# An encoder layer on one core: the MLP of 1,024 tokens as one chunk in two passes instead of two chunks of 512 in one

## The chip, the cores and the metric

The kernel runs on one core of one Trainium2 chip. The metric is the device time of one execution in microseconds (us), taken over several runs; lower is better. The core has a matrix engine (TensorE, in the profile PE for matmuls and PEld for weight loads), VectorE (DVE), ScalarE (ACT), GpSimd (POOL), and SyncE (SP), whose queue issues nearly all DMAs here. Data sits in SBUF (128 partitions), matmuls accumulate in PSUM (eight banks of 512 fp32 columns), and everything larger goes to DRAM.

## The reference

One layer of an encoder, applied to a prompt of 512 tokens and a sample of 1,024 tokens with the same weights, in fp32. Cut to the part that the change touches:

```
def _layer(h, ...):
    ...                                   # norm, projection, attention and pooling, output projection
    m = _rmsnorm(h, norm_mlp_g)           # h: tokens x 1024
    h = h + jnp.square(jax.nn.relu(m @ w_up)) @ w_down      # w_up 1024 x 4096, w_down 4096 x 1024
    gate = jax.nn.sigmoid(_rmsnorm(h, norm_ple_g) @ w_ple_gate)
    h = h + gate * (p_i @ w_ple_proj)     # then a final norm
```

## The kernel before

The 1,536 tokens are three chunks `c` of 512: chunk 0 is the prompt, chunks 1 and 2 are the sample. After attention come the MLP (about 548 to 1,574 us of the profile) and the gate with the final norm.

**Numbers in two parts.** Every fp32 operand of a large matmul is split: a high part, rounded by a ScalarE copy to the type fp32r that TensorE takes, and a low part, the rest, made by a subtraction on VectorE or GpSimd. A product then takes three matmuls (high by high, high by low, low by high; `three`, L103).

**Seven products for eight.** Both MLP products use Winograd's form of Strassen's scheme: each operand is cut into four blocks, and seven products of sums and differences of blocks give the four blocks of the result. `UP` and `DOWN` (L1204) are the orders in which the seven are taken.

**First product** (`m @ w_up`, relu, square). The 4,096 columns of `w_up` are 16 pairs `g` of 256; `pairs` (L1209) is a list of 48, chunk by chunk. The token side is cut in halves, so the moving operand of each matmul has 256 columns. The combinations of `m` are made once per chunk (`make_m`, L678), stored in DRAM (`mo_d`), and read back by `load_mo` (14 tiles per chunk). A pair's weight combinations are made by `Pair.feed` (L949) from the raw weights. Chunk 0 makes them for all 16 pairs and stores those of 15 (`KEPT`) in `kept_d`; chunks 1 and 2 read them back (`fetch`, L945) and make them only for pair 0. `Pair.product` (L991) is one product of 12 matmuls; `run7` (L1065) is a pair of chunk 1 or 2: seven products, with PSUM results combined on VectorE and ScalarE (`sc.copy(t, x)`, `u2`, `u4`, the relus and squares) into the tiles `X` of a `Double`.

**Second product.** For chunk 0 it is a plain product (`Pair.down`, L999: four pieces per pair, each of 12 matmuls of 512 columns), run by `between` one pair late. For chunks 1 and 2 two pairs make a `Double` (L1112) with seven products in Strassen's form (`down`, L1171: 24 matmuls of 256 columns, into `d0` or `d1`, two PSUM banks each); `weights` (L1128) makes the combinations of `w_down` anew for each of the 16 doubles, `inputs` (L1153) those of `X`. A double's results are added to the running sums `HS` by VectorE (`out`, L1188, the row L1196 of the profile).

**The order.** One loop over `pairs` (L1620) writes out the order. After each of a pair's products `after(i)` (L1649) takes one step of the weight stream `feeding`, of `inputs` and of `weights`, and one `step` of the side work in `chores` (squares and norms, `make_m`, `finishing`, `raise_late`, `gating`). For chunks 1 and 2, after every second product of pair n one product of the double before is put into the PE order; its sums are taken by `flush`. So first and second product of a chunk alternate on PE. PE, ACT, DVE and POOL run in the order of the program; SP's DMAs are ordered by a scheduler, but a `load` (L55) not before its turn in PE's order. Tiles come from a pool of 49 slots of SBUF (`NSLOT`, L32); a new tile waits until one is free.

**After the MLP.** `gate` (L1699) runs for chunk 0, chunk 1, and chunk 2 in two halves. Chunk 0's gate alternates on PE with the last double's products (`next_down`).

Of the kernel before, what the change touches and what calls it, by code (L numbers as in the profile page):

```python
# [18 lines left out]
P = 128  # L19
# [16 lines left out]
def encoder_layer(ctx, tc, xT, xn, xr, pT, w1, w2, w_pool, w_out, w_up, w_down, w_gate, w_proj,  # L36
# [587 lines left out]
    def rsqrt_rows(parts, w, name):  # L624
# [11 lines left out]
        if name in ("g0", "g1"):  # L636
            yield
# [14 lines left out]
        if name in ("g0", "g1"):  # L652
            yield from wait(2)
# [3 lines left out]
        yield from wait({"f20": 4, "g2": 8, "f00": 7, "f10": 4}.get(name, 3))  # L657
# [6 lines left out]
    wr_d = dram.tile([P, CH], F32, name="wr_d")  # L664
# [13 lines left out]
    def make_m(c, et, el):  # L678
# [15 lines left out]
        for b in range(2):  # L694
# [17 lines left out]
            def keep(i, j, out, b=b):  # L712
                sy.dma_start(mo_d[c][i][j][:, 2 * b:2 * b + 2], as32(out[:, j]))
                if j:
                    made.add((c, i, b))
# [19 lines left out]
        if c == 2:  # L735
            sy.dma_start(wr_d, acc[:, 1])
# [6 lines left out]

    def load_mo(c, i):
# [3 lines left out]
        for j in range(2):  # L748
            load(as32(MO[c, i][j]), mo_d[c][i][j])
# [7 lines left out]

    def quarters(t):
        return t.rearrange("p (a b) -> p a b", b=HF)

    def scaled(c, nm, a):
        t = quarters(HS[c][nm][:, a * CH:(a + 1) * CH])
        ve.tensor_tensor(t, t, ws[c][:, TOK[nm[1]]].unsqueeze(1).to_broadcast([P, 2, HF]), op=ALU.mult)

    def rest(c, nm):
        r = slot([P, D], F32, f"rest{c}{nm}")
        for a in range(2):
            load(quarters(r[:, a * CH:(a + 1) * CH]), h_d[c][2 * (int(nm[0]) - 1) + a][:, :, TOK[nm[1]]])
        return r
# [10 lines left out]
    HALVES = (slice(0, CH), slice(CH, D))  # L780

    def raise_late(c):
        w = slot([P, CH], F32, f"wr{c}")
        load(w, wr_d)
        r = {}

        def fetch(nm):
            r[nm] = rest(c, nm)
            yield

        def scale(nm):
            for part in HALVES:
                t = quarters(r[nm][:, part])
                ve.tensor_tensor(t, t, w[:, TOK[nm[1]]].unsqueeze(1).to_broadcast([P, 2, HF]), op=ALU.mult)
                yield

        def add(nm):
            for part in HALVES:
                gp.tensor_tensor(HS[c][nm][:, part], HS[c][nm][:, part], r[nm][:, part], op=ALU.add)
                yield  # L800

        yield from staged(("22", "11", "12", "21"), fetch, scale, add)

    def squares(c, acc):

        sqs = {}

        def square(nm):
            sqs[nm] = slot([P, 4, HF], F32, f"sqh{c}{nm}")
# [1091 lines left out]
```

## Time and profile before

| | |
|---|---|
| time, median of 3 runs | 1727.47 us (1727.32 to 1727.59) |
| the profiled execution: its time | 1728.79 us |
| its span, first to last instruction | 1726.5 us |
| PE busy | 1713.6 us (99%) |
| DVE, ACT, POOL busy | 1253.0, 888.9, 1073.5 us (73%, 51%, 62%) |
| granted TensorE clock, mean | 0.997 of full |
| DMA | 400.69 MB, mean 232 GB/s |

The rows shown below come from several views of this one profiled execution. The page gives totals per engine. A row of the groups reads: line, engine, operation, tiles out<-in, shapes, count | busy time together, mean ns of one | idle time before them and what ended it. A row of the timeline reads: start, duration, engine, line, operation, count of neighbours that were merged. A row of the stages gives, for a stretch of time, each engine's busy time and instruction count, then the granted clock, the DMA engines' share and the rate. Matmuls overlap in the pipeline (the listed mean is a latency), so the price of one is read from the distance between starts, not from its duration.

### The profile page before, as it was taken

What the parts mean: (1) busy time and instruction counts of PE and PEld (TensorE: products, weight loads), DVE (VectorE), ACT (ScalarE), POOL (GpSimd) and SP (SyncE); (2) the same over time, 40 slices, a digit from 0 to 9 for tenths busy, and PEclk for the clock granted to TensorE, in tenths of its full rate; (3) what the DMA queues carried; (4) which work ended last, traced back from release to release, by engine and by line L of the source; (5) the groups of instructions that cost most, each with busy time, mean ns of one, the idle gap of its engine ahead of it and who ended that gap; (6) DMA issues with size and microseconds to landing.
All of it is one profiled execution on the core that took longest, in us unless ns stands there. A gap on an engine that the chain in (4) does not pass through costs nothing.

```text
span 1726.5 us, 31311 instructions
## 1 busy us (share of the span) xinstructions
PE 1713.6 (99%) x11716; PEld 1573.6 (91%) x11716; DVE 1253.0 (73%) x1724; ACT 888.9 (51%) x1607; POOL 1073.5 (62%) x871
## 2 busy tenths in 40 slices
PE   9999999999999999999999999999999999999998
PEld 7888888888889888888999999999999999998898
DVE  6776765788887568777657778777778788665665
ACT  6444355667884546555435455544454445543233
POOL 2495983534666656777547877776688675653522
PEclk9999999999999999999999999999999999999998
DMA  7464655120429986979797778799777789743012
GB/s 260 144 220 168 238 185 194 37 99 14 151 109 356 322 299 246 391 264 370 274 394 287 265 276 319 260 330 354 264 238 267 261 328 388 267 167 116 13 50 98
DMA packets 137495, 400.69 MB, mean 232 GB/s; under 512 B 14592, under 2 KB 27264, under 8 KB 137344
## 3 DMA queue, kind: packets, MB, share of 16 engines
q1 hardware_dynamic: 136784, 398.30, 63.2%
q8 instruction: 93, 1.52, 0.4%
q14 instruction: 58, 0.48, 0.1%
q10 hardware_dynamic: 560, 0.40, 0.1%
HBM read 280.41 MB, written 118.23 MB: 231 GB/s over the span
## 4 chain that ended last, share of the span: by engine, by line
PE 55%; DMA 4%; DVE 4%; ACT 1%; issue 1%; POOL 1%; POOLq 0%; SPq 0%; DVEq 0%; ACTq 0%
PE pd L49 25%; PE pz L49 7%; PE px L49 7%; PE pq L49 7%; PE pg L49 5%; PE py L49 3%; PE pj L49 1%; DMA kept_d<-w 1%; DMA mo<-mo_d 1%; DMA rest<-h_d 1%; DMA we<-in_w_down_dram 1%; DVE h L1769 1%; DMA w<-kept_d 1%; DMA mo_d<-mm 0%; DVE s L1735 0%
## 5 line engine op out<-in xcount | busy, mean ns | idle before, releaser
L49 PE MATMUL pd<-ta,v 128*128 128x256 f32 x2688 | 337.9, 282 | 0.1
L49 PEld LDWEIGHTS pd<-ta,v 128*128 128x128 f32 x2688 | 327.9, 189 | 0.7 <-POOL v L1145 0.3
L1145 POOL TENSOR_TENSOR v<-we,v 128x512 fp32r<-128x512 f32 x128 | 185.4, 1469 | 91.0 <-DVE ta L1165 30.0
L1145 POOL TENSOR_TENSOR v<-vs,v 128x512 fp32r<-128x512 f32 x96 | 130.9, 1385 | 102.2 <-DVE c L1168 33.7
L49 PE MATMUL pd<-r,wd 128*128 128x512 f32 x768 | 189.3, 394 | 0.9 <-DVE r L1062 0.9
L49 PE MATMUL z<-w,x 128*128 128x512 f32 (+1 forms) x864 | 173.6, 358 | 0.0
L536 POOL TENSOR_SCALAR pr<-pr,rr 128x1024 f32<-128x1024 f32 (+1 forms) x96 | 94.5, 984 | 126.5 <-DVE rr L534 67.4
L49 PEld LDWEIGHTS pd<-r,wd 128*128 128x128 f32 x768 | 139.8, 188 | 29.9 <-DVE r L1062 2.1
L49 PEld LDWEIGHTS z<-w,x 128*128 128x128 f32 x864 | 143.2, 189 | 25.5 <-ACT w L163 0.6
L1165 DVE TENSOR_TENSOR ta<-c,ta 128x512 fp32r<-128x512 f32 x112 | 112.7, 1006 | 73.7 <-ACT ta L1163 62.3
L956 POOL TENSOR_TENSOR w<-ws,w 128x512 fp32r<-128x512 f32 x72 | 104.5, 1452 | 94.3 <-ACT w L955 86.4
L49 PE MATMUL px<-mo,w 128*128 128x256 f32 x1152 | 152.9, 282 | 0.0
L49 PE MATMUL pq<-mo,w 128*128 128x256 f32 x1152 | 152.5, 281 | 0.3 <-DMA w<-kept_d 0.2
L49 PE MATMUL pz<-mo,w 128*128 128x256 f32 x1152 | 152.3, 281 | 0.4 <-DVE u L1092 0.4
L49 PEld LDWEIGHTS pz<-mo,w 128*128 128x128 f32 x1152 | 145.4, 189 | 3.8 <-DVE u L1092 0.6
L49 PEld LDWEIGHTS px<-mo,w 128*128 128x128 f32 x1152 | 144.7, 189 | 2.2 <-ACT u L1077 0.6
L49 PEld LDWEIGHTS pq<-mo,w 128*128 128x128 f32 x1152 | 143.1, 189 | 1.0 <-issue 0.7
L49 PE MATMUL pg<-hg,wg 128*128 128x512 f32 (+1 forms) x768 | 141.1, 338 | 0.3 <-DVE hg L1487 0.3
L546 ACT CAST pt<-tp 128x512 fp32r<-128x512 f32 x160 | 88.0, 590 | 100.9 <-PE tp L53 100.2
L49 PEld LDWEIGHTS pg<-hg,wg 128*128 128x128 f32 x768 | 119.3, 188 | 17.1 <-DVE hg L1487 0.5
L547 DVE TENSOR_TENSOR pt<-tp,pt 128x512 fp32r<-128x512 f32 x160 | 104.1, 683 | 40.9 <-ACT pt L546 40.8
L520 DVE TENSOR_REDUCE nm<-S 128x1 f32<-128x1024 f32 (+1 forms) x96 | 100.2, 1043 | 26.6 <-PE S L49 26.1
(272 smaller groups left out, 3512.4 us busy)
## 6 DMA issues: line engine op xcount, KB each, us to landing
w<-kept_d SPq DMA_DIRECT2D x210, 512.0 KB, 5.9
kept_d<-w SPq DMA_DIRECT2D x105, 512.0 KB, 4.7
we<-in_w_down_dram SPq DMA_DIRECT2D x64, 512.0 KB, 6.7
mo_d<-mm SPq DMA_DIRECT2D x84, 256.0 KB, 6.2
mo<-mo_d SPq DMA_DIRECT2D x42, 512.0 KB, 10.2
wur<-in_w_up_dram SPq DMA_DIRECT2D x36, 512.0 KB, 6.5
wdr<-in_w_down_dram SPq DMA_DIRECT2D x32, 512.0 KB, 6.3
h_d<-h SPq DMA_DIRECT2D x16, 512.0 KB, 2.9
```

What stands on the lines that cost most here:

```text
L49: last_pe[0] = nc.tensor.matmul(*a, **k).ins
L520: ve.tensor_reduce(nm, S[:, :nch * CH], axis=AX.X, op=ALU.max, negate=True)
L536: gp.tensor_scalar(p, p, rr, 1.0, op0=ALU.mult, op1=ALU.mult)
L546: sc.copy(self.pt[kt][:, 0], tp)
L547: ve.tensor_tensor(self.pt[kt][:, 1], tp, as32(self.pt[kt][:, 0]), op=ALU.subtract)
L956: gp.tensor_tensor(t[:, 1], x, as32(t[:, 0]), op=ALU.subtract)
L1145: ins = gp.tensor_tensor(lo[:, p], src[:, p], as32(hi[:, p]), op=ALU.subtract).ins
L1165: last_ve[0] = ve.tensor_tensor(t[:, 1], x, as32(t[:, 0]), op=ALU.subtract).ins
L1769: ve.scalar_tensor_tensor(h, h, gfin_sb[:, 2 * a + e:2 * a + e + 1], r, op0=ALU.mult, op1=ALU.mult)
```

## The change

Chunks 1 and 2 become one of 1,024 tokens. Its halves are the old chunks, so every moving operand has 512 columns, and the number of matmuls halves: per pair still 7 products of 12, but 16 pairs instead of 32; 8 doubles instead of 16, each with 14 calls of `down` (7 products, two halves `a`) of 12 matmuls.

- `make_wide` replaces `make_m(1)` and `make_m(2)`, runs beside chunk 0's MLP, and stores its combinations in `mw_d`; `load_wide` reads 28 tiles during the last pair of chunk 0 in place of 14.
- `kept_d`, `fetch` and `KEPT` go; `feed_wide` makes the weight combinations for the 16 wide pairs.
- All 16 wide pairs run first (`run_wide`), with no second product between them. `Pair.inputs` makes the combinations of each pair's result and stores them in `T_d` (112 stores of 512 KB).
- Then the 8 doubles run alone. `load_t` reads the combinations back two products ahead (112 loads of 512 KB); `weights` runs 8 times instead of 16. Each `down` is followed by the sum of the one before it.
- Chunk 0's sums are stored (`sum_d`) after the wide chunk's first pair and finished beside the doubles; `stat(1)` and `stat(2)` run beside the gates of chunk 0 and 1. Chunk 0's gate has no products between its pieces any more.

The core of the diff:

```diff
+    def make_wide():
...
+    def load_wide(i):
+        all_ = [(b, j) for b in range(2) for j in range(2)]
...
+        MO[1, i] = {x: slot([P, 2, CH], F32R, f"mw{i}{x[0]}{x[1]}") for x in all_}
+        for b, j in all_:
+            load(as32(MO[1, i][b, j]), mw_d[i][b][j])
...
-        def fetch(self, i):
-            self.w[i] = slot([P, 2, CH], F32R, f"w{self.id}_{i}")
-            load(flat(self.w[i]), kept_d[self.g, i])
...
+        def run_wide(self, after):
+
+            c1, c2 = self.X = [slot([P, 2, CH], F32, f"c{self.id}{i}") for i in range(2)]
+            x = tp_ps(f"px{self.id}")
             self.product(1, x)
-            flush()
-            sc.copy(t, x)
+            sc.copy(c1[:, 1], x)
             after(1)
-            y = bank("u", "py")
+            y = ps("u", f"py{self.id}")
             self.product(6, y)
-            flush()
-            ve.tensor_tensor(u2, y, t, op=ALU.add)
+            ve.tensor_tensor(c2[:, 0], y, c1[:, 1], op=ALU.add)
             after(6)
...
+        def inputs(self):
+
+            b11, b12, b21, b22 = (x[:, i] for x in self.X for i in range(2))
+            diffs = {1: (b11, b12, b11), 3: (b12, b22, b12), 7: (b11, b22, b11), 6: (b21, b21, b11)}
+            for i, x in ((1, b11), (5, b11), (2, b21), (3, b22), (7, b12), (6, b11), (4, b21)):
+                t = slot([P, 2, CH], F32R, f"ta{self.id}_{i}")
+                sc.copy(t[:, 0], x)
+                yield
+                ve.tensor_tensor(t[:, 1], x, as32(t[:, 0]), op=ALU.subtract)
+                if i in diffs:
+                    out, y, z = diffs[i]
+                    ve.tensor_tensor(out, y, z, op=ALU.subtract)
+                later(3, load, T_d[self.g, i], flat(t))
+                yield
...
+        def load_t(self, i):
+            self.t[i] = [slot([P, 2, CH], F32R, f"tb{self.id}_{i}{p}") for p in range(2)]
+            for p in range(2):
+                load(flat(self.t[i][p]), T_d[2 * self.m + p, i])
...
+        def down(self, i, a):
+
+            fresh = i in (1, 5, 6, 7)
+            if fresh:
+                pd = ps(f"d{a}", f"pd{self.id}{i}{a}")
...
-    doubles = [Double(c, m) for c in (1, 2) for m in range(NG // 2)]
+    doubles = [Double(m) for m in range(NG // 2)]
...
-    pairs = [Pair(c, g) for c in range(3) for g in range(NG)]
+    pairs = [Pair(c, g) for c in range(2) for g in range(NG)]
...
         def after(i):
-            next(feeding, None)
+            k = UP.index(i)
+            for _ in range(1 + ((n, k) in MORE)):
+                next(feeding, None)
             next(splits, None)
...
+            if n == NG - 1:
+                load_wide(i)
+            if n == NG and k % 2 == 0:
+                before.down(k // 2)
+                later(4, load, sum_d[k // 2], hT[0][k // 2])
+            if n > NG:
+                if k or n > NG + 1:
                     next(inputs)
-                if feed_w:
-                    next(weights)
+                next(inputs)
...
+    load_ms(0)
+    chores.extend([wait(12), finishing(0)])
+    AHEAD = 2
+    for n, db in enumerate(doubles):
+        if n == 1:
+            chores.extend([raise_late(1), raise_late(2), gating(0)])
+        if n == len(doubles) - 1:
+            chores.append(first_weights())
+        for k in range(14):
+            i, a = DOWN[k // 2], k % 2
+            pending.append(db.down(i, a))
+            if len(pending) > 1:
+                pending.popleft()()
+            nxt = k // 2 + AHEAD
+            to = db if nxt < 7 else doubles[n + 1] if n + 1 < len(doubles) else None
+            if a == 0 and to:
+                to.load_t(DOWN[nxt % 7])
...
+            next(weights, None)
+            next(inputs, None)
...
+            step()
...
-            if c == 0 and d < 6:
-                next_down(d + 1)
```

More of the change, by code (lines that the diff above doesn't have):

```diff
@@ L826, in stat_h @@
-    def stat_h(c, e):
-        acc = slot([P, 2, CH], F32, f"sqg{c}")
-        def lower(nm):
-            for a, part in enumerate(HALVES):
-                t = HS[c][nm][:, part]
-                if nm != "11":
-                    e.tensor_tensor(t, t, HS[c]["u"][:, part], op=ALU.add)
-                scaled(c, nm, a)
-                yield
-        yield from staged(("11", "21", "12", "22"), lower, *squares(c, acc))
-        yield from wait(20)
+        yield from staged(range(4), fetch, idle, scale, add)
@@ L868, in spill @@
     def spill(c):
-        yield from wait(16 if c == 2 else 0)
+        yield from wait(4 if c == 2 else 0)
         for a in range(4):
@@ L956, in split @@
                 gp.tensor_tensor(t[:, 1], x, as32(t[:, 0]), op=ALU.subtract)
-                if keep:
-                    later(3, load, kept_d[self.g, i], flat(t))
             (a11, a12), (a21, a22) = ((r[:, 0:CH], r[:, CH:D]) for r in self.raw)
@@ L1214, in stream @@
+    NG, heavy = NF // 2, [False]
+    U = {}
+    E_LOADS = {0: (0, 0), 1: (0, 1), 2: (1, 1), 3: (1, 0)}
+    D_LOADS = {4: (0, 0), 6: (0, 1), 8: (1, 1), 10: (1, 0)}
+    UP, DOWN = (1, 6, 2, 5, 7, 3, 4), (1, 2, 5, 3, 7, 4, 6)
+    doubles = [Double(m) for m in range(NG // 2)]
+    T_d = {(g, i): dram.tile([P, D], F32, name=f"T_d{g}_{i}") for g in range(NG) for i in UP}
+    pairs = [Pair(c, g) for c in range(2) for g in range(NG)]
     def stream():
-        def ahead(n):
-            if n < len(pairs) and not kept(pairs[n]):
-                pairs[n].load_up()
@@ L1232, in encoder_layer, with all_inputs, all_weights @@
     feeding = stream()
-    def stream_down(kind):
+    def all_inputs():
+        for pr in pairs[NG:]:
+            yield from pr.inputs()
+    def all_weights():
         for db in doubles:
-            yield from getattr(db, kind)()
-    weights, inputs = stream_down("weights"), stream_down("inputs")
+            yield from db.weights()
+    inputs, weights = all_inputs(), all_weights()
     unit = Unit(0, 0, 0)
@@ L1689, in encoder_layer @@
+            if n == len(pairs) - 2 and k > 2:
+                doubles[0].load(*E_LOADS[k - 3])
+            if n == len(pairs) - 1:
+                if k in (3, 5):
+                    doubles[0].load_t(DOWN[k // 4])
+                if k > 2:
+                    next(weights)
+            step(c == 1 or i not in ((1, 4, 2) if heavy[0] else (1,)))
+        if c:
+            pair.run_wide(after)
         else:
@@ L1780, in bank @@
         return (ps_u("u", name) if banks[0] % banks[1] < 2 else ps_g("g", name))
-    def next_down(d):
-        flush()
-        pending.append(double.down(DOWN[d]))
-        for stream in (inputs, weights, inputs, weights):
-            next(stream, None)
-    next_down(0)
     while not fed:
```

462 lines of the change are left out of this document (204 added, 258 removed).

## The prediction

> **What bounds the kernel now.** I read the page's engine totals first, then the stages, then the PE groups of the stage that changes.
>
> ```profile
> span 1726.5 us, 31311 instructions
> PE 1713.6 (99%) x11716; PEld 1573.6 (91%) x11716; DVE 1253.0 (73%) x1724; ACT 888.9 (51%) x1607; POOL 1073.5 (62%) x871
> ...
> core 0: us, PE busy (x) PEld busy (x) DVE busy (x) ACT busy (x) POOL busy (x), PEclk, DMA share, GB/s
> 907.00:1507.00 600.00, 599.27 (x5030) 597.54 (x5029) 458.40 (x517) 301.52 (x495) 433.03 (x302) 1.00 0.81 292
> ```
>
> PE is busy 99% of the span; from 907 to 1507 us, the MLP of chunks 1 and 2, it misses 0.73 of 600 us at full clock. Only less PE time helps, and only if the other engines, at 458 and 433 of 600 us, still keep up. What a matmul costs here:
>
> ```profile
> L49 PE MATMUL pd<-ta,v 128*128 128x256 f32 x2472 | 310.7, 282 | 0.0
> L49 PE MATMUL px<-mo,w 128*128 128x256 f32 x732 | 97.4, 282 | 0.0
> L49 PE MATMUL pz<-mo,w 128*128 128x256 f32 x721 | 95.5, 281 | 0.4 <-DVE u L1092 0.4
> L49 PE MATMUL pq<-mo,w 128*128 128x256 f32 x720 | 95.2, 281 | 0.3 <-DMA w<-kept_d 0.2
> L49 PE MATMUL py<-mo,w 128*128 128x256 f32 x363 | 48.2, 282 | 0.0
> L49 PE MATMUL ssg<-ones_sb,sqg 128*128 128x1 f32 x16 | 1.9, 240 | 0.0
> L49 PE MATMUL bcg<-dgg,ones_sb 128*128 128x512 f32 x4 | 1.3, 396 | 0.0
> L49 PE MATMUL w<-sh,ones_sb 128*128 128x512 f32 x2 | 0.6, 390 | 0.0
> ```
>
> These are that stage's PE groups: 5,008 matmuls of 256 columns, and 3.8 us of others. (600 - 3.8) / 5,008 = 119.0 ns each, small stalls included. For 512 columns the nearest work is chunk 0's second product, then the gate; starts are in the first column of the timeline:
>
> ```profile
> 880.53 2.92 PE L49 MATMUL pd<-r,wd 128*128 128x512 f32 x12
> 883.29 1.57 PE L49 MATMUL px<-mo,w 128*128 128x256 f32 x12
> ...
> 895.91 2.94 PE L49 MATMUL pd<-r,wd 128*128 128x512 f32 x12
> 898.69 1.58 PE L49 MATMUL pz<-mo,w 128*128 128x256 f32 x12
> ...
> 1580.32 1.55 PE L49 MATMUL pj<-pp,wpj 128*128 128x512 f32 x6
> ...
> 1587.23 1.55 PE L49 MATMUL pj<-pp,wpj 128*128 128x512 f32 x6
> ```
>
> Twelve take 2.76 and 2.78 us, and the gate's 30 take 6.91: 230 to 232 ns. So two narrow ones cost 238 and one wide one about 231; seven ns are paid per instruction, not per column.
>
> **The change part by part.** *Matmuls.* Chunks 1 and 2 have 32 pairs x 84 and 16 doubles x 168, together 5,376 narrow matmuls: x 119.0 ns = 640 us. After: 16 x 84 + 8 x 168 = 2,688 wide ones x 231 ns = 621 us. Gain 19 us; at 230 ns 22, at 233 ns 14.
>
> The Trainium skill, "TensorE: Matmul & The Clock Gate", section "Back-to-back issue gap", gives columns / 2.4 + 2.5 ns for an isolated gap; by it a merged pair saves only 2.5 ns, an estimate of 7 us in all. The rows here show 7 ns for a pair, so the measurement decides.
>
> *Work of the other engines.* Added: 14 more feeds (32 instead of 18), each seven POOL subtractions, seven ACT casts, four DVE sums. Removed: half the `w_down` combinations (112 POOL subtractions, 56 casts, 32 sums of 1,024 columns). Prices:
>
> ```profile
> L1145 POOL TENSOR_TENSOR v<-we,v 128x512 fp32r<-128x512 f32 x128 | 185.4, 1469 | 91.0 <-DVE ta L1165 30.0 <-DVE c L1168 16.4 <-ACT v L1139 15.7
> L956 POOL TENSOR_TENSOR w<-ws,w 128x512 fp32r<-128x512 f32 x72 | 104.5, 1452 | 94.3 <-ACT w L955 86.4 <-issue 7.2
> L1165 DVE TENSOR_TENSOR ta<-c,ta 128x512 fp32r<-128x512 f32 x112 | 112.7, 1006 | 73.7 <-ACT ta L1163 62.3 <-POOL sqg L1524 3.1 <-issue 2.7
> L1168 DVE TENSOR_TENSOR c<-c,c 128x512 f32<-128x512 f32 x48 | 43.1, 898 | 0.0
> L975 DVE TENSOR_TENSOR ws<-wur,ws 128x512 f32<-128x512 f32 x18 | 20.4, 1133 | 0.0
> L964 DVE TENSOR_TENSOR ws<-wur 128x512 f32<-128x512 f32 x18 | 17.3, 963 | 0.0
> L547 DVE TENSOR_TENSOR pt<-tp,pt 128x512 fp32r<-128x512 f32 x160 | 104.1, 683 | 40.9 <-ACT pt L546 40.8
> L1196 DVE TENSOR_TENSOR H<-pd,H 128x1024 f32<-128x1024 f32 x72 | 87.5, 1215 | 5.1 <-PE pd L49 5.1
> L1142 DVE TENSOR_TENSOR vs<-vs,we 128x1024 f32<-128x1024 f32 x16 | 26.0, 1628 | 0.0
> L1108 ACT ACTIVATE c<-c 128x512 f32<-128x512 f32 x32 | 20.2, 630 | 35.7 <-DVE c L1107 35.6
> ```
>
> POOL: +98 x 1.45 - 112 x 1.47 = -22 us. DVE: +56 x 1.0 - 32 x 1.63 = +4 us. The totals hardly move; what changes is where they fall, so each stage needs its own account.
>
> *First wide product.* A pair has 7 x 2.77 = 19.4 us of PE. In it DVE does seven `ta` (7.0), four differences (3.6; the one of product 1 is now among them), four weight sums (about 4.0) and five sums out of PSUM at 0.68 (3.4): 18.0 us, 93%. POOL does seven at 1.45: 10.2. No product of the second kind lies between any more to cover a late VectorE. The tightest place is the pair's end: after product 4 come a DVE sum (0.68), relu and square of 1,024 columns (two 512-column halves each by L1108, 2.5), two casts (1.3) and the copy of the next pair's `px` (0.6), 5.1 us in a row, while PE has two products (5.5 us) before it needs that copy. That leaves 0.4 us for DVE to be late. Lower bound 0; upper bound 0.7 us late in each of 15 pairs, 11 us. I take 2 us, near the low end, because of this stretch of chunk 0, where POOL is as full:
>
> ```profile
> 696.00:717.00 21.00, 21.00 (x134) 18.88 (x133) 15.95 (x17) 11.99 (x23) 19.92 (x14) 1.00 1.01 365
> ```
>
> PE is unbroken there with POOL at 19.92 of 21. It bears on `make_wide` too. DVE and POOL slow each other: alone, an SBUF subtraction takes 0.68 on DVE and 1.27 on POOL,
>
> ```profile
> 1117.51 0.68 DVE L1165 TENSOR_TENSOR ta<-c,ta 128x512 fp32r<-128x512 f32 x1
> ...
> 1132.27 2.55 POOL L1145 TENSOR_TENSOR v<-vs,v 128x512 fp32r<-128x512 f32 x2 [1.37 <-ACT mm L725]
> ```
>
> against means of 1.0 and 1.45. Laid end to end at these alone-times, the stretch 696:717 holds 13 to 14 POOL operations and 8 of DVE without PSUM (its 17 less nine sums out of PSUM): 22 to 23 us in 21. A wide pair has 7 and 15: 19.1 in 19.4.
>
> *make_wide in chunk 0.* A block's seventeen heavy steps carry 14 POOL and 8 DVE subtractions, four steps a pair: 3.3 and 1.9 on top of the pair's own 9 and 8. End to end 15.6 + 6.7 = 22.3 us in a pair of 21.05, for 8.5 pairs. The stretch above shows as much hidden, so 0; upper bound 8.5 x 1.3 = 11.
>
> *The 28 tiles.* 28 x 524 kB = 14.7 MB are read between the first product of chunk 0's last pair (near 864 us) and the last product of the first wide pair, 44.5 us later (19.6 + nine pieces of 2.77).
>
> ```profile
> 862.00:883.00 21.00, 21.00 (x133) 18.95 (x132) 14.07 (x17) 10.03 (x20) 12.76 (x10) 1.00 0.96 358
> 883.00:904.00 21.00, 21.00 (x133) 18.97 (x133) 8.81 (x12) 6.81 (x14) 7.08 (x6) 1.00 1.03 408
> ...
> w<-kept_d SPq DMA_DIRECT2D x210, 512.0 KB, 5.9
> kept_d<-w SPq DMA_DIRECT2D x105, 512.0 KB, 4.7
> mo<-mo_d SPq DMA_DIRECT2D x42, 512.0 KB, 10.2
> ```
>
> At 408 GB/s that is 36 us, so the rate suffices. Slots are tighter: by my count of live tiles the 28, the pair's weights (5), raw weights, sums and results (6 to 8) and what chunk 0 still holds (sums 4, `wd` 4, `r` 2, squares 3) reach 49 to 52 of 49. The last loads may wait for the stores of `sum_d`, and SP's later DMAs behind them. 0 to 9 us (a store of 4.7, a load of 10.2, less 5.5 in hand); I take 2.
>
> *Second wide product.* Per piece of 2.77 us DVE has a sum of 1.215, half a weight sum (0.47 on average: four of 1.63 per double) and under 0.4 of side work: 2.1. PE reuses a bank one piece later, so a sum may be 1.5 us late. `finishing` makes DVE wait one step after it asks for its first tiles: 5.9 - 2.8 = 3.1, or 1.6 beyond that slack. Tiles of `T_d` come two products, 11 us, ahead of use. 0 to 8 us (1 us a double); I take 2. DMA falls: 315 transfers of `kept_d` go, 224 of `T_d` come.
>
> *Gates and tail.* Same matmuls; `stat` runs beside the gates, where DVE is idle a third of the time:
>
> ```profile
> 1580.00:1638.00 58.00, 58.00 (x262) 47.48 (x261) 37.04 (x49) 20.55 (x30) 25.82 (x21) 1.00 0.11 33
> ```
>
> I take 0, from -1 to +3.
>
> **Sum.** -19 + 2 + 0 + 2 + 2 = -13 us on a span of 1726.5: 1713.5, and 2.3 us outside it as now. The profiled execution (1728.79) stands 1.3 us over the median 1727.47; from the median the sum gives 1714.5, rounded 1714.
>
> **The rivals.** *Slots or loads at the joint of chunk 0 and the wide chunk.* It costs its upper 9 us instead of 2, and a little of it recurs in the first pairs, where `ta` tiles wait for their stores: 1723. For: the count of live tiles. Against: 408 GB/s today without a PE gap.
>
> *DVE becomes the bound of the first wide product* (slower). Besides 18.0 us of work, each `ta` waits for its cast: row L1165 has 62.3 us of that over 112, 0.6 each, 4.2 a pair. If none of it overlaps, a pair takes 22.2 instead of 19.4: 15 x 2.8 = 42 us, so 1714 - 2 + 42 = 1754. The gain is gone once DVE needs more than 20.3 us a pair. Against: those waits happen while DVE is ahead of PE, and the casts are now issued one product earlier.
>
> *POOL and DVE exclude each other fully.* Then `make_wide` costs its 11 us: 1725, no change that can be measured. Against: 22 to 23 us fitted in 21.
>
> The Trainium skill states this lock in "SBUF — State Buffer", section "SBUF: two separate sides": whoever starts first holds the shared port pair for the whole instruction. The slow means agree, the stretch 696:717 says it is not quite whole.
>
> *A matmul of 512 columns costs 235 ns or more in the new order:* the gain shrinks to 8 us and, with the stalls, 1726.
>
> **How the numbers follow.** Forecast 0.63, joint 0.14, both faster; full exclusion 0.05 and dear wide matmuls 0.04, no change; DVE bound 0.12 and a stall that I do not see 0.02, slower. Under 0.2% (3.5 us) a measurement can't tell from no change: faster 0.77, same 0.09, slower 0.14. Range: 1706 (22 us gained, no stall) to 1727 holds all but the slower cases and a little of the others. The likeliest case alone: 1707 to 1720.
>
> **What would show it.** Right: `pd`, `px` to `pq` with 512 columns, 2,688 of them, starts 2.77 us apart per dozen; a wide pair every 19.4 us; a double every 38.8; PE busy near 1,700 us. Wrong: PE gaps released by DVE or ACT at the second product of each wide pair; by DMA `mw` tiles near 890 us; by DVE `H` in the doubles; a dozen at 2.82 or more.

## The result, and the profile after

The changed kernel takes 1736.41 us (median of four runs, 1735.07 to 1738.15) against 1727.52 us: a ratio of 1.0052, 95% interval 1.0035 to 1.007. It is slower by about 9 us, where 13 us less were forecast. A second set of runs gave 1735.32 us, 1.0042 (1.0029 to 1.0054).

The profiled execution of the changed kernel took 1735.07 us, 6.8 us of span more than before. First the heads of its page: matmuls fell from 11,716 to 9,028 and busy PE time from 1713.6 to 1704.3 us, but the idle time, span less PE, grew from 12.9 to 29.0 us.

```profile
span 1733.3 us, 25333 instructions
PE 1704.3 (98%) x9028; PEld 1437.7 (83%) x9028; DVE 1279.5 (74%) x1683; ACT 869.1 (50%) x1515; POOL 1052.5 (61%) x844
```

The stages tell where. A row gives start:end and length in us, the busy time of PE, PEld, DVE, ACT and POOL, then the clock, the DMA share and GB/s. This is the table of busy time by stretch, of before (chunk 0's MLP; chunks 1 and 2 with gate 0; gate 1):

```profile
548.40:883.30 334.90, 333.81 (x2117) 300.64 (x2116) 240.35 (x290) 181.25 (x340) 231.37 (x160) 1.00 0.86 317
883.30:1594.10 710.80, 709.98 (x5687) 695.67 (x5686) 521.72 (x592) 341.61 (x560) 481.99 (x337) 1.00 0.77 280
1594.10:1652.30 58.20, 58.20 (x262) 47.63 (x261) 36.43 (x50) 18.35 (x29) 26.59 (x24) 1.00 0.03 10
```

and of after (chunk 0; the wide first product, with chunk 0's last four down pieces; the doubles; gate 0; gate 1):

```profile
550.60:892.20 341.60, 335.24 (x2114) 299.75 (x2113) 247.08 (x287) 196.10 (x346) 275.79 (x186) 1.00 0.53 182
892.20:1220.20 328.00, 325.92 (x1397) 260.99 (x1397) 284.59 (x318) 194.03 (x326) 174.10 (x116) 1.00 0.69 257
1220.20:1540.30 320.10, 316.34 (x1356) 254.50 (x1355) 214.97 (x187) 87.89 (x99) 213.31 (x149) 0.99 0.86 329
1540.30:1597.20 56.90, 56.90 (x251) 46.30 (x250) 33.86 (x43) 20.97 (x32) 27.61 (x21) 1.00 0.20 65
1597.20:1657.70 60.50, 58.65 (x260) 47.06 (x259) 48.07 (x63) 21.47 (x33) 27.95 (x22) 1.00 0.11 44
```

Chunk 0, whose matmuls did not change, takes 341.6 us instead of 334.9. Chunks 1 and 2 with gate 0 take 328.0 + 320.1 + 56.9 = 705.0 instead of 710.8: 5.8 us gained where 19 were forecast before stalls. Gate 1 loses 2.3, what follows it 1.4 (75.6 for 74.2). The remaining 2.2 us lie ahead of the MLP, which starts at 550.6 instead of 548.4; in the second set's trace it starts at 548.6, so that part is no effect of the change. There chunk 0 took 343.1 us, 8.2 more than before; the 1.5 us beyond 6.7 are a spell of half clock, of which the last section tells.

What PE waited for, by stretch, from the table of waits of after: chunk 0 (first row), the wide first product (second), the doubles (two rows), the gates (two rows). Columns: who waits and for whom, us in total, times, longest; "issue" is a wait for nothing that the profile shows.

```profile
PE pd L49 <- DVE r L1129: 5.8, 7, 1.5
...
PE px L49 <- ACT c L1137: 1.4, 3, 0.9
...
PE pd L49 <- ACT Hu L1241: 2.0, 1, 2.0
PE pd L49 <- issue: 1.0, 2, 0.5
...
PE ssf L49 <- POOL s L1743: 3.0, 2, 1.7
PE bcf L49 <- DVE dgf L655: 1.1, 2, 0.8
```

This table leaves out the smallest gaps. Measured from start to start, PE loses 5.3 us behind the copy of `px` at 14 of the 15 joints of wide pairs, most of them 0.2 to 0.3 us.

How the largest in chunk 0 comes about is seen in VectorE's timeline of after. Product 3 of this pair of chunk 0 is complete near 669.4 us; the sum `c<-pz` that frees its bank and feeds relu, squares and `r` starts at 672.00.

```profile
666.85 0.68 DVE L784 TENSOR_TENSOR t<-m,m 128x512 f32<-128x512 f32 x1
667.46 0.41 DVE L1113 TENSOR_TENSOR c<-pq,u 128x256 f32<-128x256 f32 x1
667.79 1.45 DVE L1030 TENSOR_TENSOR ws<-wur 128x512 f32<-128x512 f32 x1
669.16 1.78 DVE L784 TENSOR_TENSOR t<-m,m 128x512 f32<-128x512 f32 x1
670.86 1.21 DVE L1080 TENSOR_TENSOR h02m<-pd,h02m 128x1024 f32<-128x1024 f32 x1
672.00 0.41 DVE L1117 TENSOR_TENSOR c<-pz,u 128x256 f32<-128x256 f32 x1
672.33 0.68 DVE L1032 TENSOR_TENSOR ws<-ws,wur 128x512 f32<-128x512 f32 x1
672.93 0.68 DVE L784 TENSOR_TENSOR m<-m,m 128x512 f32<-128x512 f32 x1
```

L784 are `make_wide`'s differences. Four fall into this pair (three here, one at 659.23), 0.68 us alone and 1.78 beside a GpSimd instruction. The pair's own short sums stand behind them in the queue, and 3.5 us later PE waits 0.33 and then 1.73 us for `r`. VectorE is only 72% busy in this stretch (247 of 342 us); it has time left, and still these sums come late.

### The profile page after: what moved, and what is told of

Read it like the earlier page. It is cut to its first block, busy times and chain, and to the rows that moved or that the text cites. A ratio compares the mean times of both kernels' runs of the same rounds, so it can differ in the third digit from the quotient of the medians.

```text
span 1733.3 us, 25333 instructions
## 1 busy us (share of the span) xinstructions
PE 1704.3 (98%) x9028; PEld 1437.7 (83%) x9028; DVE 1279.5 (74%) x1683; ACT 869.1 (50%) x1515; POOL 1052.5 (61%) x844
## 4 chain that ended last, share of the span: by engine, by line
PE 38%; DVE 7%; ACT 3%; issue 1%; POOL 1%; DMA 0%; POOLq 0%; ACTq 0%; DVEq 0%
PE pd L49 18%; PE px L49 5%; PE pz L49 4%; PE pq L49 4%; PE pg L49 3%; PE py L49 2%; PE pj L49 1%; DVE ta L1174 1%; DVE hg L1520 1%; DVE s L1735 1%; DVE H L1736 1%; ACT s L1734 1%; DVE c L1177 1%; DVE h L1769 0%; ACT ta L1172 0%
## 5 line engine op out<-in xcount | busy, mean ns | idle before, releaser
L49 PE MATMUL pd<-tb,v 128*128 128x512 f32 x1344 | 315.5, 396 | 3.8 <-ACT Hu L1241 2.0
L49 PEld LDWEIGHTS pd<-tb,v 128*128 128x128 f32 x1344 | 253.2, 189 | 65.4 <-ACT Hu L1241 2.4
L1010 POOL TENSOR_TENSOR w<-ws,w 128x512 fp32r<-128x512 f32 x128 | 185.0, 1450 | 155.5 <-ACT w L1009 155.5
L1010 POOL TENSOR_TENSOR w<-wur,w 128x512 fp32r<-128x512 f32 x96 | 154.3, 1620 | 65.9 <-ACT w L1009 62.0
L1212 POOL TENSOR_TENSOR v<-we,v 128x512 fp32r<-128x512 f32 x80 | 117.9, 1498 | 69.8 <-ACT v L1206 49.7
L1243 DVE TENSOR_TENSOR H<-pd,H 128x1024 f32<-128x1024 f32 x72 | 87.8, 1222 | 71.1 <-PE pd L49 71.1
L1172 ACT CAST ta<-c 128x512 fp32r<-128x512 f32 x112 | 69.3, 620 | 107.8 <-DVE c L1177 107.0
L530 ACT ACTIVATE pr<-S,nm 128x1024 f32<-128x1024 f32 (+1 forms) x96 | 94.2, 981 | 12.4 <-DMA qs_d<-qs 6.3
L49 PE MATMUL px<-mw,w 128*128 128x512 f32 x384 | 95.3, 397 | 1.6 <-ACT c L1137 1.4
L49 PE MATMUL o<-pt,vs 128*128 128x512 f32 x320 | 93.2, 403 | 0.8 <-DVE pt L547 0.8
```

The costliest lines, as they stand in the source:

```text
L49: last_pe[0] = nc.tensor.matmul(*a, **k).ins
L530: sc.activation(self.pr[j], S[:, :n], AF.Exp, bias=nm, accum_out=self.sums[:, j:j + 1])
L1010: gp.tensor_tensor(t[:, 1], x, as32(t[:, 0]), op=ALU.subtract)
L1172: sc.copy(t[:, 0], x)
L1212: gp.tensor_tensor(lo[:, p], src[:, p], as32(hi[:, p]), op=ALU.subtract)
L1243: ve.tensor_tensor(H[at], pd, H[at], op=ALU.add)
```

## The experiments

All edits are to the changed kernel. Stretches run from PE start to PE start: chunk 0, wide first product, doubles, gate 1, and the first half of chunk 2's gate (2a). The row after_again is the changed kernel itself; ratios are to the kernel before in the same set of runs. Rows with the same code in chunk 0 differ there by up to 2.9 us (341.5 to 344.4); the last section says why.

| run | chunk 0 | wide | doubles | gate 1 | gate 2a | us | ratio, 95% |
|---|---|---|---|---|---|---|---|
| before | 334.9 | - | - | 58.1 | 31.6 | 1727.4 | |
| after_again | 343.1 | 328.0 | 320.9 | 60.5 | 34.6 | 1735.32 | 1.0042, 1.0029-1.0054 |
| c0_no_subs | 335.0 | 327.8 | 320.2 | 60.3 | 34.5 | 1726.41 | 0.9992, 0.9982-1.0001 |
| c0_low_act | 335.4 | 328.4 | 319.5 | 60.4 | 33.1 | 1725.96 | 0.9990, 0.9981-0.9999 |
| c0_subs_pool | 345.2 | 328.1 | 320.1 | 60.4 | 33.1 | 1735.59 | 1.0046, 1.0032-1.0060 |
| c0_shift | 347.5 | 328.1 | 318.9 | 60.3 | 34.6 | 1737.81 | 1.0063, 1.0051-1.0076 |
| c0_spread | 346.5 | 341.5 | 318.8 | 60.4 | 34.6 | 1750.08 | 1.0133, 1.0117-1.0148 |
| wider_nocalm | 352.7 | 327.9 | 317.7 | 60.4 | 31.1 | 1740.88 | 1.0071, 1.0059-1.0083 |
| hu_first | 344.4 | 328.0 | 318.2 | 60.3 | 34.5 | 1733.03 | 1.0033, 1.0020-1.0045 |
| inputs_later | 344.2 | 328.0 | 325.9 | 60.5 | 34.5 | 1740.04 | 1.0076, 1.0063-1.0088 |
| scale_stat | 343.0 | 327.8 | 322.0 | 66.6 | 29.7 | 1739.46 | 1.0075, 1.0063-1.0088 |
| relu_late | 342.9 | 366.3 | 322.7 | 60.5 | 32.9 | 1776.92 | 1.0283, 1.0269-1.0298 |
| inputs_pool | 341.6 | 427.5 | 317.3 | 60.3 | 34.6 | 1832.73 | 1.0603, 1.0589-1.0617 |
| px_calm_tail | 341.5 | 353.4 | 320.5 | 60.6 | 31.5 | 1758.68 | 1.0180, 1.0166-1.0194 |
| three_fixes | 344.3 | 328.0 | 322.4 | 60.5 | 31.1 | 1733.23 | 1.0024, 1.0012-1.0036 |
| we_sooner | 341.6 | 327.9 | 322.4 | 60.4 | 31.1 | 1735.48 | 1.0046, 1.0034-1.0058 |

**Chunk 0: which work costs the 8 us.** The theory was `make_wide`'s work on VectorE; the rivals were GpSimd's lower parts, ScalarE's casts, and transfers. First the change once more, to see which parts repeat:

> The changed kernel itself once more, as a base for the others. Late engines (VectorE and ScalarE reach PE's operands late at fixed places of the program): the same gaps at the same places, chunk 0's MLP 341 to 342 us, the wide first product 328, the doubles 320, 1735 to 1738 us in all. Loads and slots: the gaps move from run to run. The 2.2 us that it lost before the first attention score (183.75 against 181.54 us) comes back at another size if it is chance of the run, and at the same size if it is the program.

The losses of chunk 0, the wide product, the doubles and the gates all came back within 1.5 us; only the late start did not. Then the differences moved to GpSimd:

```
-    ve.tensor_tensor(o[:, h], x[:, h], y[:, h], op=ALU.subtract)   # make_wide, sub()
+    gp.tensor_tensor(o[:, h], x[:, h], y[:, h], op=ALU.subtract)
```

> make_wide's sixteen half-tile subtractions go from VectorE to GpSimd; all else as changed. If chunk 0's MLP lost its 6.7 us because VectorE reaches the end of a pair late: it falls from 341.6 to 335 to 337 us and the time by 4 to 6 us. If it lost them to the port that both engines share: a subtraction holds it 1.27 us on GpSimd in place of 0.68, the load end to end rises from 22.3 to 23.5 us a pair, and the stage gets longer, 343 us or more. Loads and slots: no change.

Chunk 0 did not recover: 345.2 us. PE's waits for `r` stayed (5.6 us for 5.8), and 3.1 us for GpSimd's weight tiles joined them. Two runs leave work out, one side each, so that their results are not the layer's. c0_no_subs drops the calls of `sub`, and with them the tile `t2`:

```
-                if t_:
-                    sub(int(t_), int(t_ % 1 * 2))
```

> Leaves the 16 differences of make_wide on VectorE (0.68 us each, or more beside GpSimd) out of the computation; casts, GpSimd's differences, loads and stores stay as they are. If VectorE's own work is what makes the chain at the pair's end late, chunk 0 falls from 343 us to 335-337, as before the change, and the whole by 6 to 8 us, to 1728. If it is GpSimd's differences or ScalarE's casts of make_wide, or its transfers, chunk 0 stays at 341 us or more.

c0_low_act drops GpSimd's lower parts and keeps `sub`; ScalarE copies of the same size write those tiles:

```
-    gp.tensor_tensor(out[i][1][:, h], of[i][:, h], as32(out[i][0][:, h]), op=ALU.subtract)
+    sc.copy(out[i][1][:, h], of[i][:, h])
```

> Leaves the 28 differences for the lower parts of make_wide on GpSimd (1.3 to 1.7 us each) out of the computation: copies on ScalarE, of the same size, write those tiles instead. VectorE keeps its 16 differences. If chunk 0's loss is the number of VectorE instructions alone, chunk 0 stays at 341 us or more. If it is VectorE and GpSimd slowing each other (a difference of 128x512 takes 0.68 us on VectorE alone and up to 1.78 beside GpSimd), chunk 0 falls from 343 us to 335-338 and the whole to 1727-1730 us.

The table of busy time for chunk 0, in the order c0_no_subs, c0_low_act, c0_subs_pool (columns as above: length, then PE, PEld, DVE, ACT, POOL):

```profile
549.60:884.60 335.00, 333.77 (x2115) 300.07 (x2114) 236.07 (x271) 196.44 (x346) 271.41 (x186) 1.00 0.53 185
...
548.50:884.00 335.50, 334.29 (x2116) 300.00 (x2115) 238.37 (x288) 210.80 (x374) 229.79 (x158) 1.00 0.53 186
...
549.60:894.80 345.20, 336.13 (x2115) 299.83 (x2114) 236.58 (x271) 195.54 (x346) 294.55 (x202) 1.00 0.51 179
```

Either removal restores the 335 us of before; moving the differences across does not. With GpSimd at 271 us and no differences PE is as unbroken as before, with the differences and GpSimd at 230 too, and with both it is not. Transfers (the DMA share is 0.51 to 0.53 in all) and ScalarE's casts, which stayed in both runs, are excluded as the sole cause, and so is the number of VectorE instructions alone. Is it the two engines slowing each other? At the two longest waits, yes. In the pair shown above, the difference at 669.16 starts behind a lower part of `make_wide` on GpSimd (first row, of after) and takes 1.78 us. In c0_low_act GpSimd is idle at that place: the difference takes 0.68 us, and `c<-pz` follows within 0.2 us of product 3's end near 667.0, not 2.6 us after it (the other rows):

```profile
668.65 1.74 POOL L777 TENSOR_TENSOR mm<-m,mm 128x512 fp32r<-128x512 f32 x1
...
665.40 0.68 DVE L784 TENSOR_TENSOR t<-m,m 128x512 f32<-128x512 f32 x1
...
667.14 0.41 DVE L1117 TENSOR_TENSOR c<-pz,u 128x256 f32<-128x256 f32 x1
```

The difference gives 1.1 of these 2.4 us, earlier instructions of VectorE the rest. The pair with the other long wait, at 830 us, shows the same. Together the two pairs hold 4.2 of the 6.7 us. Yet the slowing alone does not cost it: `r` itself takes 0.93 us on average from 640 to 880 us in after, 0.72 in c0_low_act (0.76 before), but 0.92 in c0_no_subs, where PE does not wait. So in these pairs it takes both, the differences in VectorE's queue and GpSimd's lower parts beside them; for the smaller waits, and for c0_subs_pool, the way is not shown.

Three edits tried to find room by place or size. c0_shift lets heavy steps run beside products 6, 2, 5, 7 instead of 6, 5, 7, 3:

```
-    step(c == 1 or i not in ((1, 4, 2) if heavy[0] else (1,)))
+    step(c == 1 or i not in ((1, 4, 3) if heavy[0] else (1,)))
```

> The heavy steps of make_wide run beside products 6, 2, 5 and 7 of a pair of chunk 0 instead of 6, 5, 7 and 3: the same instructions, none of them now issued in the last third of a pair, just ahead of the chain (add, relu, squares, difference) whose end the second product of that pair waits for. If the loss of chunk 0 is a matter of place in the in-order queues (VectorE's late differences at the pair's end, ScalarE's casts ahead of the last relu), chunk 0 falls from 343 us to 335-338 and the whole by 4 to 8 us, to 1728-1731. If it is the sheer amount of work on VectorE and GpSimd that is too much for these pairs, the waits only move to another place of the pair and chunk 0 stays within 2 us of 343. If stores and loads were at fault, nothing changes either.

c0_spread issues a difference only beside products 6 and 5, at most two to a pair; the other steps come in a new order and beside product 2 too:

```
+    if subs and heavy[1] in (6, 5) and set(needs[subs[0][0]]) <= done:
+        x = subs.popleft()
+        sub(*x)
...
-    step(c == 1 or i not in ((1, 4, 2) if heavy[0] else (1,)))
+    step(c == 1 or i not in ((1, 4) if heavy[0] else (1,)))
```

> make_wide keeps all its instructions, but its 16 differences on VectorE are now issued at most two to a pair of chunk 0, beside products 6 and 5 alone, between steps that hold only casts and GpSimd's differences (these may now also stand beside product 2). If the 9 us that the differences cost come from their bunching (up to four in one pair, the last just ahead of the chain at the pair's end), chunk 0 falls from 343 us to 336-339 and the whole to 1728-1731. If the pairs of chunk 0 have no room for them at any place (VectorE and GpSimd share their time too tightly), chunk 0 stays at 341 us or more and the whole at 1734-1737.

Both were worse than the change: 347.5 and 346.5 us. New waits appeared where the differences now stood. From the table of waits of c0_spread:

```profile
PE px L49 <- ACT c L1155: 11.9, 3, 10.9
PE pq L49 <- DVE c L1131: 4.6, 4, 1.5
```

L1131 is VectorE's sum of `pq` after product 7, for which product 4 waits. And `make_wide` ended later, so that in the wide product PE stood 10.9 us for the first copy of `px` (L1155), which had to wait behind a cast of ScalarE that waited 14.7 us for a store of `make_wide`. Last, differences and lower parts as instructions of 128x1024:

```
-    ve.tensor_tensor(o[:, h], x[:, h], y[:, h], op=ALU.subtract)
+    if h:
+        ve.tensor_tensor(o, x, y, op=ALU.subtract)      # and the lower part likewise
```

> Only the first double's copies ahead of its casts, the loop without the background queue, and the differences as instructions of 128x1024; the doubles' background steps and loads stand where the change put them. Doubles 318 us as in the run with the first edit alone, gates 2 to 3 us less, chunk 0 341-342 if engine time is the cause: 1728-1730 us; 1731 us if chunk 0 stays.

The differences took less time (14.1 us for 19.7), GpSimd in all too (267 for 276), VectorE in all a little more (250 for 247); chunk 0 grew to 352.7 us, with two waits of 2.85 us for `r`, start to start, and 4.9 us of half clock behind them. The same edit with the others of we_sooner gave 352.4 and 1741.93 us (wider, 1.007, 1.0056 to 1.0084):

> As the run with the weights loaded sooner, and make_wide's differences as 8 instructions of 128x1024 on VectorE and 14 on GpSimd in place of 16 and 28 of 128x512 (1.21 for two of 0.68 us; 2.4 for two of 1.3). If the loss of chunk 0 is engine time, it falls by 1 to 2 us of 8, to 341-342; if fewer and longer instructions are worse, because VectorE's instruction waits for a whole one of GpSimd's, chunk 0 grows to 345 us or more. With the loads' theory right, 1724-1728 us in all.

So the loss does not follow the engine time of the side work. Longer instructions cost more; this run lengthens those of both engines and can't tell them apart. GpSimd's 2.82 us each show on VectorE: `ws<-wur` takes 1.94 us on average from 640 to 880 us, where after has 1.46.

**The wide first product.** The prediction named the pair's end, where ScalarE's copy of `px` comes late. It does: 1.04 us at 969, 0.5 at 948. Its timeline in after:

```profile
966.51 1.06 ACT L1162 ACTIVATE c<-c 128x1024 f32<-128x1024 f32 x1 [0.73 <-DVE c L1161]
967.60 1.06 ACT L1163 ACTIVATE c<-c 128x1024 f32<-128x1024 f32 x1
968.57 0.60 ACT L1009 CAST w<-ws 128x512 fp32r<-128x512 f32 x1
969.08 0.61 ACT L1172 CAST ta<-c 128x512 fp32r<-128x512 f32 x1
969.60 0.57 ACT L1137 COPY c<-px 128x512 f32<-128x512 f32 x1
```

Two experiments took work out of the copy's way. relu_late puts relu and square of `c2` after the next pair's copy:

```
     self.product(1, x)
     sc.copy(c1[:, 1], x)
+    while late:
+        late.pop()()                 # relu and square of the last pair's c2
```

> In the wide first product the relu and square of the last two blocks are emitted on ScalarE behind the next pair's copy of px, not ahead of it. Late engines: the gap before each pair's second use of px (py to px, 0.13 to 1.04 us, some 4 us over the stage) is gone, the stage falls from 328 to 324 us. Loads and slots: the gaps stay.

px_calm_tail (its first edit; it also holds a broadcast of rows, `f00`, back by four steps, and has two edits shown below) takes the cast of `ta` out of the pair's last step and issues it beside products 2 and 7:

```
-    if k or n > NG + 1:
-        next(inputs)
-    next(inputs)
+    for _ in range(0 if k == 6 else 3 if k in (2, 4) else 2 if k or n > NG + 1 else 1):
+        next(inputs)
```

> Three edits in three stretches. (1) First wide product: no cast of a pair's inputs is issued between the square of c2 and the next pair's copy of px. If the 0.2 to 1.0 us waits for that copy are ScalarE's queue order, the stretch falls from 328.0 to 325-326 us; if ScalarE is late for VectorE's differences, it stays. (2) Doubles after the first: the background steps are taken out of the half products in which the weights' sums run on VectorE and put into others. If the four waits of 0.6 to 1.15 us there are the sums out of PSUM, queued behind both, they go and the stretch falls from 320.9 to 317-318 us; if they are transfers, they stay. (3) Gates: the loop that waits for the third chunk's statistics no longer runs the background queue, and the broadcast of the second chunk's rows comes 4 steps later. If these bursts make the waits of 1.84 and 0.94 + 0.56 us, they go: 2 to 3 us. All three: 1727-1729 us; none: 1735 us.

Both made it much worse: 366.3 and 353.4 us. From the tables of waits of relu_late from 934 to 1200 us (PE, then ScalarE), and ScalarE's of after:

```profile
PE px L49 <- ACT c L1137: 17.7, 12, 1.5
PE py L49 <- POOL w L1010: 7.2, 12, 0.6
...
ACT ta L1173 <- DVE c L1178: 114.9, 35, 4.6
...
ACT ta L1172 <- DVE c L1177: 96.3, 28, 4.6
```

ScalarE was not busy but blocked: the cast of the next `ta` needs a difference of VectorE (L1178, L1177 in after), and everything behind it in the queue waits along, the copy of `px` and the casts of `w` too. The change has that wait as well (last row), but not just ahead of the copy: there relu and square stand (rows at 966.51 and 967.60). inputs_pool tests what happens when this difference comes later:

```
-    ve.tensor_tensor(out, y, z, op=ALU.subtract)      # Pair.inputs, four to a pair
+    gp.tensor_tensor(out, y, z, op=ALU.subtract)
```

> The four differences for each pair's inputs of the second products (64 of 0.69 us in all) run on GpSimd instead of VectorE. VectorE is busy for 244.5 of 266 us from 934 to 1200 us, GpSimd for 146.5. Theory: VectorE's queue is what makes the 4 us of small waits in the first wide product; then VectorE falls to some 205 of 266 us, the stretch from 328.0 to 324-325 us and the whole by 3 to 4 us. Rival: the casts on ScalarE wait for each difference in turn, and GpSimd needs 1.3 us for one and stands behind the weights' lower parts; then ScalarE's copies come later still, and the stretch grows to 332 us or more.

The waits of PE and of ScalarE, 934 to 1300 us, and the busy time of 934 to 1200 us, of this run and then of after:

```profile
PE px L49 <- ACT c L1137: 65.3, 13, 6.0
...
ACT ta L1172 <- POOL c L1177: 177.7, 54, 4.6
...
934.00:1200.00 266.00, 214.64 (x825) 169.75 (x824) 143.38 (x164) 123.20 (x206) 159.73 (x111) 0.88 0.48 181
...
934.00:1200.00 266.00, 263.92 (x1130) 210.78 (x1129) 244.08 (x274) 165.03 (x279) 147.18 (x96) 1.00 0.65 243
```

That is 427.5 us: VectorE is free (143 of 266 us against 244 in after), and PE waits 5 us a pair, with half clock after each wait (0.88 of full clock on average). No engine is full; the chain cast, lower part, difference, cast seems to set the pace, with the difference now in GpSimd's queue behind the weights' lower parts. four_fixes, the same with the three edits below, gave 1834.54 us (1.0608, 1.0590 to 1.0626):

> The three edits outside chunk 0 together with the pairs' differences on GpSimd. If VectorE's queue is the cause of the first wide product's waits, 1721-1723 us; if GpSimd is too slow for them, 1728 us or more.

**The doubles and gates.** The first wait, 2.16 us from 1225.5 on, is for ScalarE's copy of the first bank behind two casts:

```profile
1224.19 1.06 ACT L1163 ACTIVATE c<-c 128x1024 f32<-128x1024 f32 x1
1225.41 0.62 ACT L1172 CAST ta<-c 128x512 fp32r<-128x512 f32 x1 [0.15 <-DVE c L1177]
1225.93 1.04 ACT L1206 CAST v<-vs 128x1024 fp32r<-128x1024 f32 x1
1226.88 1.00 ACT L1241 COPY Hu<-pd 128x1024 f32<-128x1024 f32 x1
```

Putting off the last pair's inputs to the second double:

```
+            if n:
                 next(inputs, None)
```

> The last wide pair's combinations are made beside the second double instead of the first. Late engines: the first double's 2.16 us gap (ScalarE comes to its first PSUM copy late, behind casts) falls below 0.7 us, the halved clock after it (seven matmuls of 427 ns, 1.4 us) does not come, and the doubles take 316 to 317 us instead of 320. If the gap comes from the loads of tb instead, it stays.

It did not go (2.13 us), since a cast of `ta` and one of `v` still stood there (1225.99 and 1226.52 us), and a wait of 2.5 us for `ta` joined it in the second double. hu_first puts the loop's cast of `ta` behind the first two copies; it also issues `weights` one product sooner:

```
-            next(weights, None)
-            next(inputs, None)
+            if n or k:
+                next(weights, None)
+            for _ in range((k > 1) + (k in (5, 9)) if n == 0 else 1):
+                next(inputs, None)
```

> In the first double, the casts for the weights (1.04 us) and of the last pair's inputs (0.62 us) are no longer issued ahead of the first two copies out of PSUM: weights start one step earlier, beside the last pair, and the inputs make up their two steps at the sixth and tenth half product. If the wait of 2.1 us for the first copy Hu, and the half clock that follows it (some eight matmuls at 427 ns, 1.5 us), come only from ScalarE's order at this place, the stretch of doubles falls from 320.9 us to 317-318 and the whole by 3 to 4 us, to 1731-1732. If ScalarE is late there because VectorE's sums for the last pair are late, or the tiles of double 0 are, the wait stays over 1 us and the time within 1.5 us of 1735.

Doubles 318.2 us, 2.7 less than in after_again: a cast of `ta` and one of `v` still ran ahead of the first copy (1225.49 and 1226.00 us), and the wait shrank only to 1.63 us, but the half clock behind it went (last section). scale_stat gave raise_late's products to GpSimd, let chunk 2's statistics wait six steps less and the broadcast `f00` four more:

> Two edits in two stretches. (1) raise_late multiplies on GpSimd instead of VectorE (16 of 0.68 us): if the small waits of the doubles after the first (1301 to 1435 us, some 4 us in sum) are late sums on VectorE, the stretch of doubles falls by 2 to 3 us; if they are casts on ScalarE or the tiles' loads, it stays. (2) the statistics of chunk 2 wait 6 steps less before the rows' rsqrt: if the 1.84 us wait for the statistics' first matmul in the middle of the second gate's last chunk is the burst of steps that are run out there at once, this wait goes below 0.5 us and that stretch falls from 33-34.6 us to 32. Together 1731-1732 us; with neither, 1735.

The doubles grew by 1.1 us, by one wait of 4.4; gate 2a fell to 29.7 but gate 1 rose to 66.6, where the matmuls of the statistics now came before GpSimd's sums were ready (2.3 us). The burst of steps in the gate went by another edit, which px_calm_tail, wider_nocalm, wider, four_fixes and the runs below share; gate 2a fell to 31 us without a loss in gate 1:

```
     while c not in bcs:
-        step()
+        step(c < 2)
```

three_fixes joins this, hu_first, and another distribution of background steps over the doubles' half products:

```
-            step()
+            step(1 if n == 0 else {1: 0, 2: 0, 4: 2, 6: 2, 8: 2, 10: 0, 12: 0, 13: 2}.get(k, 1))
```

> Three edits to the changed kernel outside chunk 0 and the first wide product: the first double's two copies out of PSUM ahead of its casts; the background steps of the later doubles moved out of the half products in which the weights' sums run on VectorE; and the loop that waits for the third chunk's statistics no longer runs the background queue. Theory: the waits of the doubles and of the second gate's end are late VectorE and ScalarE work, and each goes without a new one elsewhere. Then the doubles fall from 320.9 us to 313-314 and the second gate's first half from 34.6 to 31.5, and the whole to 1724-1726 us, just below the kernel before, although chunk 0 still takes 343 us. Rival: the background steps are needed where they stand, and their delay comes back as one long wait (over 4 us), as one did beside the same step table earlier: 1729-1731 us.

Eleven of its twelve runs fell into two groups, six at 1728.7 to 1731.4 us and five at 1735.1 to 1736.7 (the twelfth, 2071 us, stands alone); the traced one is of the second. In it one VectorE instruction lasted 8.32 us; the timeline of VectorE, then of GpSimd:

```profile
1322.96 1.22 DVE L1243 TENSOR_TENSOR H<-pd,H 128x1024 f32<-128x1024 f32 x1 [1.50 <-PE pd L49]
1324.10 8.32 DVE L864 TENSOR_TENSOR rest<-rest,wr 128x512 f32<-128x512 f32 x1
1332.34 1.21 DVE L1243 TENSOR_TENSOR H<-pd,H 128x1024 f32<-128x1024 f32 x1
...
1324.37 2.59 POOL L1212 TENSOR_TENSOR v<-vs,v 128x512 fp32r<-128x512 f32 x2
1326.88 4.99 POOL L1212 TENSOR_TENSOR v<-we,v 128x512 fp32r<-128x512 f32 x4
```

It ends 0.55 us after GpSimd's unbroken row; PE stood 5.3 us for the bank that the next sum frees. we_sooner took away the late load that ran ahead of this row:

```
-    D_LOADS = {4: (0, 0), 6: (0, 1), 8: (1, 1), 10: (1, 0)}
+    D_LOADS = {2: (0, 0), 4: (0, 1), 6: (1, 1), 8: (1, 0)}
```

> The three edits, with each double's weights loaded two half products sooner. In the run with the three edits alone one wait of 5.3 us stood at 1328 us: ScalarE waited 7.7 us for a weights tile, GpSimd then ran six lower parts one behind another, and a VectorE multiplication of 128x512, 0.68 us elsewhere, ended 8.3 us after its start, when GpSimd's row had ended. Theory: VectorE does not get its operands as long as GpSimd's instructions follow each other without a gap, and the late load made that row; then with the loads sooner no VectorE instruction takes over 2.5 us there, the doubles fall from 322.4 us to 313-316 and the whole to 1726-1729 us. Rival: the wait comes from the loads of the inputs (all transfers ran at some 410 GB/s there), and stays: 1733 us.

The late load was not the cause of the row: with the loads sooner GpSimd works without a gap from 1311.8 to 1329.3 us, and L864, which starts at 1321.71, takes 8.15 us again. The kernel with all edits of the second kind, best1 (c0_spread, px_calm_tail, hu_first), did not have this wait, and its doubles took 313.1 us, 7.8 less than after_again; chunk 0 and the wide product, at 345.2 and 368.6, cost far more: 1769.58 us (1.0253, 1.0231 to 1.0276).

> The spread differences of chunk 0, the first double's copies ahead of its casts, and the three edits to the first wide product, the later doubles and the gates, all in one kernel. If each gives what the theory of late VectorE and ScalarE work says, 4 to 7 + 2 to 3 + 2 + 3 + 2 us, the kernel runs in 1718-1723 us, below the 1727.5 of the kernel before. If only the first double's edit holds, as measured, 1732-1733 us.

No version that computes everything was faster than the kernel before.

## Why the prediction was wrong

*Matmuls, -19 us: right.* From 1445 to 1535 us, in the doubles of after:

```profile
1445.00:1535.00 90.00, 90.00 (x390) 1.00 0.91 339
```

That is 230.8 ns for one of 512 columns, as forecast (231), wherever PE is not held up. The rival of dear wide matmuls is not borne out. Nor is the rule for an isolated gap in the Trainium skill, "TensorE: Matmul & The Clock Gate", section "Back-to-back issue gap", by which, as an estimate, only 7 us would be saved.

*make_wide at 0: the step that failed first.* It measured 6.7 us, and 8.2 with a spell of half clock, within the upper bound of 11 that the prediction kept but did not take. The reason given was that as much work, laid end to end, had been hidden in a pair before. That compares loads: 1.9 differences a pair on average, at 0.68 us each. In the pair shown there are four, one takes 1.78 us beside GpSimd, and the sum `c<-pz` behind it comes 2.6 us late although VectorE and GpSimd have time left (72% and 81% busy). Without the differences, or without the lower parts, the loss is gone.

*The 28 tiles, +2: too dear.* PE waited for none of them.

*First wide product, +2: mis-sized.* Its 1,344 matmuls at 231 ns and the four pieces of chunk 0 (48 at 231) come to 321.6 us, with the statistics' broadcast 322.2; it took 328.0, so 5.8 us, 5.3 of them behind the copy of `px`. The place was right (`px` behind ScalarE), and VectorE is at 92% of 934 to 1200 us, against 93% forecast. That it becomes the bound, the rival of 1754 us, is not what happened.

*Second wide product, +2: mis-sized.* 1,344 x 231 ns = 310.5 us; it took 320.1, so 9.6. Of these 1.3 are ten matmuls of gate 0's statistics, which lay in this stretch of the kernel before too; the loss is 8.3: 2.2 for the first copy, 1.6 for the half clock after it, 2.8 for six waits of 0.2 to 0.7, the rest spread thin. The prediction counted VectorE's average load per piece; what showed was ScalarE's order at the start, and, at two of the small waits (1336 and 1394 us), sums queued behind two instructions of side work.

*Gates, 0 (-1 to +3): 3.7 us,* above the upper end: `bcf` behind late work in gate 1, and the burst of steps in chunk 2's gate.

So in this trace the forecast -13 became +6.8 us: 19.8 us apart: 6.7 from make_wide, 7.2 in the MLP of chunks 1 and 2 (-5.8 where -19 + 6 was forecast), 3.7 in the gates and 2.2 from the start. make_wide and the first wide product stayed within their bounds, the doubles and gates passed theirs by 0.3 and 0.7 us; the range was too narrow because it let only one of them go wrong at a time. What they share, by the waits shown, is side work ahead of a chain that PE waits for; no run took it away in all stages at once.

The rival of full exclusion of GpSimd and VectorE gave 1725 us by make_wide's 11 us. It had the right place, and the two costly pairs show its mechanism at work; its size was too large by 4.3 us in this trace, and the whole time was missed, since the other stages lost too.

## What to carry to other kernels

When PE is full, price side work that is moved by where it stands in each in-order queue, and by what it meets on the other engine, not by the engines' busy shares: name the shortest chain that it stands ahead of, and that chain's slack. A cast that waits for another engine blocks all that is issued behind it, so a new place for it can cost more than the work itself. An unknown cost with the same cause in several stages belongs in the range at its upper end in all of them at once.

## What the runs showed of the hardware

*A short wait can cost twice.* After the first double's wait of 2 us the granted clock in after (length, PE's time and count, then the clock) was:

```profile
1225.00:1228.00 3.00, 1.01 (x6) 1.00 0.96 272
1228.00:1231.00 3.00, 3.00 (x9) 0.64 1.02 407
1231.00:1240.00 9.00, 9.00 (x37) 0.93 1.03 418
```

Seven starts in a row were 427 ns apart instead of 231; with the partly slow ones at the edges 1.6 us were lost beside the 2.16 of the wait. Over all traces of this study, between 548 and 1640 us, with waits measured from start to start: of 138 waits of PE of 0.85 to 1.67 us none was followed by this, of 29 of 1.69 to 1.74 us ten were, of two near 2.05 us none, of 53 of 2.1 us or more fifty, at 1.0 to 2.5 us each. The Trainium skill, "TensorE: Matmul & The Clock Gate", section "Why this matters for your kernels", asks only that PE have no idle gaps above some 3 us; here 1.7 us could be enough. Of the 2.7 us that hu_first gained, some 1.6 are this. So is the scatter of chunk 0, whose two waits of 1.7 us stand at the edge: it took 341.5 or 341.6 us in the four traces with no such spell in it, 342.9 to 343.1 in four with one, 344.2 to 344.4 in three with two.

*GpSimd can keep VectorE out for a whole row.* The Trainium skill, "SBUF — State Buffer", section "SBUF: two separate sides", says that whoever of the two starts first holds the shared ports for one whole instruction. The 1.78 us for a 0.68 us instruction agree with that, and so does this count: of VectorE's two-operand instructions of 128x512 without a tile of PSUM, all 207 in after that last over 1 us end 0.54 to 0.56 us after a GpSimd instruction's end (before: all 146). But 8.32 us span six GpSimd instructions one behind another, so VectorE did not get its turn between them. It happened in five of the traces (8.32, 8.25, 8.18, 8.15 and 7.35 us), at one place each; why not elsewhere is open.
